# Two small transformers in one launch: first block on feature-major tokens, its norm factors applied behind the products, part of the issue order pinned, weight loads four units ahead

## The chip, the cores and the metric

The kernel runs on one core of one Trainium2 chip. The metric is device time in microseconds (us) of one launch, as a median of runs. The engines are TensorE (PE, with its weight loads shown as PEld), VectorE (DVE), ScalarE (ACT), GpSimd (POOL) and SyncE (SP), which issues the loads. "Half" weights, half clock and so on are explained where they come up.

## What is computed

The first network is one block over 256 tokens of width 1024, a gated linear attention (4 heads, key width 128, value width 256) and a squared-ReLU feed-forward of width 4096. Its output is the input of the second network (two layers of latent and context streams with adaptive norms), which makes up the rest of the launch. The change is in the first network and in the hand-over to the second one's context stream:

```
def rms_norm(x, g):
    y = xf * lax.rsqrt(jnp.mean(xf * xf, axis=-1, keepdims=True) + EPS)
    return (y * g.astype(jnp.float32)).astype(x.dtype)

x = x + gla_mixer(rms_norm(x, norm_mix), ...)
x = x + sqrelu_mlp(rms_norm(x, norm_ffn), w1, w2)     # square(relu(h @ w1)) @ w2

# gla_mixer
proj = h @ w_in                                       # q, k, v, r, gk_low
log_a = log_sigmoid(gk_low @ w_gk_up + b_gk) / 16
... chunked recurrence with decay exp(cumsum(log_a)), output o per head ...
o = rms_norm(o, g_onorm)
return (o * silu(r)) @ w_out
```

A norm is a factor per token (the reciprocal root) and a factor per feature (the gain g). A product over features commutes with the factor per token.

## The kernel before, in words

All weights stream from DRAM once (some twice) as units of 128 x 1024 floats (512 KB), in the order of the list UNITS. Three helpers handle them:

- `w_load(upto)` (line 143) issues loads on SP into tiles `raw` (5 buffers, line 145).
- `w_split(upto)` (line 150) makes two rounded halves of a unit: `wh` by a cast on ACT (line 157) and `wl = raw - wh` on DVE (line 158). Both come from a pool "w" of 13 buffers.
- `wnext(kind)` (line 162) is called where a unit is used. It asks for loads up to five units past the splits (lines 166 and 169) and for splits two units ahead of use (`cap[0]` is 3).

Every wide product is three products of halves (`mm3`, lines 174 to 176): hi x hi, lo x hi, hi x lo. A unit of form "f" (features out) has 24 products over 256 tokens; a unit "r" or "h" has 12 products over 512 columns. So PE needs wh first and wl one product later.

The order of instructions on each engine is chosen ahead of time by the framework's scheduler from its own timing model, with the source order as priority; it may move an instruction past others.

The first block, in source order: x is loaded token-major (lines 120 to 126), with the identity, the gains `vc` and the gate weights `gkraw`. `normed` (line 198) squares each half on ACT (194), gets the reciprocal root on POOL (185 to 187) and scales on DVE (201). `to_T` (208 to 234) transposes on PE (214), and ACT and DVE write two halves of the feature-major tokens `xT` with the gain applied (221, 222). Then come the gate products `pg` (377), eight units f for queries and keys (383 to 391), between which stand the decay chain (398 to 408: product, absolute value, exp, log) and the decay sums (414, 416), and one step of the modulation work after each odd f. A modulation step loads 512 KB (`p`, 284) into a buffer of the pool "w" and reduces it twice on DVE (304). It belongs to the second network and is spread as filler (`adaA`, `adaB`, `adaC`).

Next are eight units of values, with one step of the attention core per unit: `level_diag`, seven levels and `level_cross` (424 to 477), each a few DVE subtractions (443, 444), two exponentials on ACT (446), multiplications (449, 450), small products on PE (457) and a masked copy (458). Two `gate_half` passes give the gates (520, 521). In the second, `heads_out` (531 to 539) makes the head outputs and `heads_T` (553 to 557) transposes them. The output projection follows (579 to 597), then the norm and the transposes of both token tiles into `hT` (595, 608) and the feed-forward: `tok_up`, and from line 671 the loop over 32 units f, with filler. In that loop the context of the second network is loaded, normed and transposed (683 to 690).

Of the kernel before, what the change touches and what calls it, by code (L numbers as in the profile page):

```python
# [16 lines left out]
P = 128  # L17
D = 1024
# [64 lines left out]
def net(ctx, tc, x, vecs, gk_w, gk_up, g_onorm, wst, final_norm, ctx_in, ada, ada_b, cvec, norm_final,  # L83
        rpb, q_gain, k_gain, cmat, cmask, out):
# [30 lines left out]

    xin = [[t2([512]) for _ in range(2)] for _ in range(NT)]
# [3 lines left out]
    for t in range(NT):  # L120
        for hf in range(2):
            nc.sync.dma_start(out=xin[t][hf], in_=x[t * P:(t + 1) * P, hf * 512:(hf + 1) * 512])
        if t == 0:
            nc.sync.dma_start(out=cm[:, C_IDENT:C_IDENT + P], in_=cmat[:, C_IDENT:C_IDENT + P])
    nc.sync.dma_start(out=vc, in_=vecs)
    nc.sync.dma_start(out=gkraw, in_=gk_w.rearrange("p (k r) -> p k r", r=16))
# [4 lines left out]
    V.tensor_copy(out=identr, in_=ident)  # L131
# [215 lines left out]
    adaB = ada_jobs([(0, v, True) for v in (3, 4, 2)])  # L347
    adaC = ada_jobs([(0, 5, True), (1, 0, True), (1, 1, True)] + [(1, v, False) for v in (3, 4, 2, 5)])


    w_load(4)
    xT = new_T()
    gkT = t2([S])
    V.memset(gkT[0:32, :], 1.0)
    xn = [normed(h) for h in xin]
# [3 lines left out]
    to_T(xn, xT, 0, vc[:, V_MIX0, :])  # L359
    nc.sync.dma_start(out=cm[:, C_TRI:C_END], in_=cmat[:, C_TRI:C_END])  # L360
    for ci in range(2):
        bcast_row(crow[ci], cvec, ci * D, D)
    nc.sync.dma_start(out=bcol, in_=ada_b)
    gkup = t2([512])[0:17, :]
    nc.sync.dma_start(out=gkup, in_=gk_up)
    masks = const([P, len(LEVELS), P], "masks", U8)
    for n in range(2):
        mf = t2([4, P])
        m = min(4, len(LEVELS) - 4 * n)
        nc.sync.dma_start(out=mf[:, 0:m, :], in_=cmask[:, 4 * n:4 * n + m, :])  # L370
        G.tensor_copy(out=masks[:, 4 * n:4 * n + m, :], in_=mf[:, 0:m, :])
    gon = t2([256])
    bcast_row(gon, g_onorm, 0, 256)
# [4 lines left out]
    A.copy(out=gkT[0:16, :], in_=pg[0:16, :S])  # L378
# [3 lines left out]
    las = []  # L382
    for f in range(8):
        u = wnext(("f", "w_in"))
        pq = bank()
        for k in range(KD):
            mm_f(pq[:, :S], u, xT, k, 0, S, k == 0, k == KD - 1)
        if f < 4:
# [3 lines left out]
        if f == 0:  # L392
            for ci in range(2):
                A.activation(out=crow[ci], in_=crow[ci], func=AF.Silu)
        if f == 1:
            pzs, es = [bank(), bank()], [t2([512]), t2([512])]
            for t in range(NT):
                T.matmul(pzs[t], lhsT=gkT[0:17, t * P:(t + 1) * P], rhs=gkup, start=True, stop=True)
        if f == 2:
            for pz, e in zip(pzs, es):  # L400
                A.activation(out=e, in_=pz, func=AF.Abs)
            for e in es:
                A.activation(out=e, in_=e, func=AF.Exp, scale=-1.0)
            for e in es:
                A.activation(out=e, in_=e, func=AF.Ln, bias=1.0)
            for pz, e in zip(pzs, es):
                la = t2([512])
                V.scalar_tensor_tensor(out=la, in0=pz, scalar=0.0, in1=e, op0=ALU.min, op1=ALU.subtract)
                las.append(la)
        if f in (4, 5):  # L410
            t = f - 4
            pb = bank()
            for h in range(4):
                T.matmul(pb[:, h * P:(h + 1) * P], lhsT=las[t][:, h * P:(h + 1) * P], rhs=tri, start=True, stop=True)
            for h in range(2):
                A.copy(out=bT[h][:, :, t * P:(t + 1) * P],
                       in_=pb[:, h * S:(h + 1) * S].rearrange("p (h t) -> p h t", h=2))
        ada_run(adaA) if f % 2 else None
# [74 lines left out]
    for k in range(KD):  # L493
        u = wnext(("r", "w_in", k))
        for t in range(NT):
            mm_r(ac[t], u, xT[k], t, k == 0, k == KD - 1)
        core_step()
    for t in range(NT):
        d = [t2([512]) for _ in range(2)]
        for hf in range(2):  # L500
            A.copy(out=d[hf], in_=ac[t][hf])
# [7 lines left out]
    def gate_half(hf, between):  # L509
# [8 lines left out]
        for t in range(NT):  # L518
            sg[t][hf] = t2([512])
            A.activation(out=sg[t][hf], in_=ac[t], func=AF.Silu)  # L520
            V.tensor_tensor(out=sg[t][hf].rearrange("p (h v) -> p h v", h=2),
                            in0=sg[t][hf].rearrange("p (h v) -> p h v", h=2),
                            in1=gon.rearrange("p (o v) -> p o v", o=1).to_broadcast([P, 2, 256]), op=ALU.mult)

    def heads_out(t):
        ms, rs = sums[t]
        for hf in range(2):
# [6 lines left out]
            for h in (2 * hf, 2 * hf + 1):  # L534
                vs = slice((h % 2) * 256, (h % 2 + 1) * 256)
                A.activation(out=ys[t][hf][:, vs], in_=po[:, vs], func=AF.Square, scale=1.0 / 16.0,
                             accum_out=ms[:, h:h + 1])
# [22 lines left out]
    while core or open_:  # L560
        core_step()

    def second(kp):
# [886 lines left out]
```

## Time and profile before

| what | before |
|---|---|
| median of 3 runs | 1293.06 us (1291.61 to 1294.86) |
| profiled execution: its time, its span | 1293.85 us, 1292.1 us |
| ACT busy | 685.1 us (53%) |
| DMA moved | 228.84 MB |
| raw loads (`raw`), modulation loads (`p`) | 310 and 96, 512 KB each |

The span runs from the first to the last instruction; the time of the execution holds the span and what lies around it. "Busy" of PE counts modelled ends of pipelined products, so products that follow each other without a gap show as one busy stretch even at half the clock; the step from one start to the next shows the speed. In a wait row, "PE b L174 <- DVE t L222: 3.4, 2, 2.1" means: the product of line 174 waited for DVE's line 222, 3.4 us in total, twice, 2.1 us the longest.

### The profile page before, as it was taken

How to read it: one execution, taken by the hardware profiler on the slowest of the kernel's cores; microseconds unless marked ns; L12 is line 12 of the kernel's file. 1: busy time of each engine (PE TensorE's matmuls, PEld its weight loads, DVE VectorE, ACT ScalarE, POOL GpSimd, SP SyncE). 2: the span in 40 equal slices, each digit the busy share in tenths (PEclk: the TensorE clock that was granted, in tenths of full speed). 3: DMA queues.
4: the chain of work that ended last, by engine and by line, in shares of the span. 5: the costliest groups of instructions: out<-in, count | busy, mean ns of one | idle time of the engine just before them, and what ended most of it. 6: DMA issues, size and time to landing. Idle time of an engine off the chain costs nothing. (4 is left out here: it accounts for less than half of the span.)

```text
span 1292.1 us, 18813 instructions
## 1 busy us (share of the span) xinstructions
PE 1256.1 (97%) x6992; PEld 1049.7 (81%) x6992; DVE 920.6 (71%) x1612; ACT 685.1 (53%) x1312; POOL 68.3 (5%) x125
## 2 busy tenths in 40 slices
PE   6999999999999999999999999999999999999997
PEld 5887788998878777789877888888888677899996
DVE  3996798787899778778656666646667877655554
ACT  5655565566538888854212312223556887644442
POOL 1000000010200000010000000000002200000001
PEclk9999999999999999999999999999999999999999
DMA  7626587877575232364755675664853133766650
GB/s 278 228 86 209 173 274 244 281 249 245 196 250 124 83 107 87 104 221 131 167 170 194 219 230 196 222 150 140 291 191 116 48 99 86 225 191 184 196 164 33
DMA packets 73454, 228.84 MB, mean 177 GB/s; under 512 B 14209, under 2 KB 14849, under 8 KB 73362
## 3 DMA queue, kind: packets, MB, share of 16 engines
q1 hardware_dynamic: 73362, 227.64, 55.9%
q8 instruction: 55, 0.90, 0.3%
q14 instruction: 37, 0.30, 0.1%
HBM read 226.54 MB, written 1.07 MB: 176 GB/s over the span
## 5 line engine op out<-in xcount | busy, mean ns | idle before, releaser
L157 ACT CAST wh<-raw 128x1024 fp32r<-128x1024 f32 x310 | 318.9, 1042 | 296.4 <-DVE mod L304 92.9
L158 DVE TENSOR_TENSOR wl<-raw,wh 128x1024 fp32r<-128x1024 f32 x310 | 372.1, 1212 | 141.8 <-PE b L175 75.6
L175 PE MATMUL b<-t,wl 128*128 128x256 f32 (+1 forms) x1120 | 366.5, 327 | 5.6 <-DVE wl L158 5.6
L174 PE MATMUL b<-t,wh 128*128 128x256 f32 (+1 forms) x1120 | 367.2, 328 | 1.5 <-ACT wh L157 1.5
L176 PE MATMUL b<-t,wh 128*128 128x256 f32 (+1 forms) x1120 | 365.6, 327 | 0.0
L174 PE MATMUL b<-wh,t 128*128 128x512 f32 x744 | 296.4, 400 | 5.0 <-DVE t L222 2.1
L175 PE MATMUL b<-wh,t 128*128 128x512 f32 x744 | 295.8, 398 | 0.4 <-DVE t L557 0.2
L176 PE MATMUL b<-wl,t 128*128 128x512 f32 x744 | 294.9, 397 | 0.0
L304 DVE CUSTOM_DVE_ANT_0 p<-p,crow 128x1024 f32<-128x1024 f32 x160 | 194.6, 1222 | 105.0 <-DMA p<-in_ada_dram 100.4
L175 PEld LDWEIGHTS b<-t,wl 128*128 128x128 f32 x1120 | 211.6, 189 | 28.9 <-DVE wl L158 7.3
L174 PEld LDWEIGHTS b<-t,wh 128*128 128x128 f32 x1120 | 211.7, 189 | 24.3 <-ACT wh L157 1.7
L176 PEld LDWEIGHTS b<-t,wh 128*128 128x128 f32 x1120 | 211.4, 189 | 20.3
L174 PEld LDWEIGHTS b<-wh,t 128*128 128x128 f32 x744 | 139.8, 188 | 36.6 <-DVE t L222 2.3
L175 PEld LDWEIGHTS b<-wh,t 128*128 128x128 f32 x744 | 140.0, 188 | 33.1 <-DVE t L1280 1.1
L176 PEld LDWEIGHTS b<-wl,t 128*128 128x128 f32 x744 | 140.0, 188 | 32.8 <-DVE wl L158 0.3
L953 ACT CAST t<-t 128x512 fp32r<-128x512 f32 (+1 forms) x42 | 21.8, 519 | 86.1 <-DVE t L947 86.1
L185 POOL TENSOR_SCALAR c<-c 128x1 f32<-128x1 f32 x22 | 10.6, 482 | 619.1 <-ACT t L194 438.7
L946 ACT ACTIVATE t<-b 128x512 f32<-128x512 f32 (+1 forms) x42 | 20.7, 493 | 42.5 <-PE b L176 42.5
L319 POOL TENSOR_TENSOR mod<-mod,bcol 128x8 f32<-128x8 f32 x20 | 13.9, 695 | 437.0 <-DVE mod L304 433.6
L194 ACT ACTIVATE t<-t 128x512 f32<-128x512 f32 x40 | 25.0, 625 | 21.5 <-DVE t L916 8.7
L954 DVE TENSOR_TENSOR t<-t,t 128x512 fp32r<-128x512 f32 (+1 forms) x42 | 23.7, 564 | 15.4 <-ACT t L953 15.4
L214 PE MATMUL b<-cm,t 128*128 128x128 f32 x144 | 23.7, 294 | 8.7 <-DVE t L201 8.1
(203 smaller groups left out, 1187.3 us busy)
## 6 DMA issues: line engine op xcount, KB each, us to landing
raw<-in_wst_dram SPq DMA_DIRECT2D x310, 512.0 KB, 4.1
p<-in_ada_dram SPq DMA_DIRECT2D x96, 512.0 KB, 4.7
t<-in_rpb_dram SPq DMA_DIRECT2D x16, 256.0 KB, 4.1
t<-row SPq DMA_DIRECT2D x12, 256.0 KB, 6.3
t<-in_ctx_dram SPq DMA_DIRECT2D x8, 256.0 KB, 6.1
t<-in_x_dram SPq DMA_DIRECT2D x4, 256.0 KB, 3.2
crow<-in_cvec_dram SPq DMA_DIRECT2D x2, 512.0 KB, 9.4
out_dram<-t SPq DMA_DIRECT2D x4, 256.0 KB, 2.3
```

The source lines that it names most:

```text
L157: A.copy(out=h[:, :n], in_=raw[:, :n])
L158: V.tensor_tensor(out=l[:, :n], in0=raw[:, :n], in1=h[:, :n], op=ALU.subtract)
L174: T.matmul(o, lhsT=lh, rhs=rh, start=first, stop=False)
L175: T.matmul(o, lhsT=ll, rhs=rh, start=False, stop=False)
L176: T.matmul(o, lhsT=lh, rhs=rl, start=False, stop=last)
L194: A.activation(out=junk[hf], in_=halves[hf], func=AF.Square, scale=1.0 / 32.0, accum_out=ms[:, hf:hf + 1])
L214: T.transpose(out=pt[:, i * P:(i + 1) * P], in_=xn[k // 4][:, (k % 4) * P:(k % 4 + 1) * P], identity=ident)
L304: V.tensor_tensor_reduce(out=raw if ci == n_c - 1 else p4([D]), in0=raw, in1=crow[ci], scale=1.0, scalar=0.0, op0=ALU.mult, op1=ALU.add, a ...
L319: G.tensor_tensor(out=m, in0=m, in1=bcol[:, L, v, :], op=ALU.add)
L946: A.activation(out=a, in_=pa[:, :n], func=AF.Silu)
L953: A.copy(out=h, in_=a)
L954: V.tensor_tensor(out=l, in0=a, in1=h, op=ALU.subtract)
```

## The change

1. Inputs get feature-major copies of x (`xt`) and of the context (`ctxt`). The block's tokens `xT` come from `xt` with the gain alone. The factors per token are computed later (`norm_factors`, after the second unit) into `rx` and applied behind the products: to the decay logits, the values (its square), the gates and the scale of the heads' squares. Queries and keys need none: the head norm behind them takes it out.
2. The decay bias is added on DVE from its own load instead of a row of ones in the product.
3. For SP, ACT and DVE the order up to the end of the eight units is the source order (`tc.manual_schedule`); after that, up to the end of the second gate half, for ACT alone.
4. Loads that the start does not need (masks, gain of the heads, `crow`, ...) move behind unit 5 (`later_operands`); the gate weights and gains are issued by ACT. Modulation steps leave the eight units; two run in the second gate half, the rest in the feed-forward loop up to f = 19. `adaB` takes its jobs in the order 2, 3, 4.
5. The feed-forward's norm: the residual itself is transposed; the squared factor is applied to the last product (ReLU squared lets it through as a square).
6. The context: two transposes make a row of factors, POOL multiplies the feature-major context by it.
7. `w_load` asks for four units past the splits instead of five. The buffers stay five.

```diff
-        w_load(max(i + 1, wpos[1]) + 5)
+        w_load(max(i + 1, wpos[1]) + 4)
...
-            w_load(wpos[1] + 5)
+            w_load(wpos[1] + 4)
...
-    adaB = ada_jobs([(0, v, True) for v in (3, 4, 2)])
+    adaB = ada_jobs([(0, v, True) for v in (2, 3, 4)])
...
+    nc.scalar.dma_start(out=gkraw, in_=gk_w.rearrange("p (k r) -> p k r", r=16))
+    nc.scalar.dma_start(out=vc, in_=vecs)
...
+    in_order = tc.manual_schedule(engines={mybir.EngineType.SP, mybir.EngineType.Activation, mybir.EngineType.DVE})
+    in_order.__enter__()
+    for n in range(KD // 2):
+        nc.sync.dma_start(out=xraw[n], in_=xt[:, 2 * n:2 * n + 2, :])
     w_load(4)
+    for t in range(NT):
+        for hf in range(2):
+            nc.sync.dma_start(out=xin[t][hf], in_=x[t * P:(t + 1) * P, hf * 512:(hf + 1) * 512])
...
-    xn = [normed(h) for h in xin]
...
-    to_T(xn, xT, 0, vc[:, V_MIX0, :])
...
     for k in range(KD):
+        src, w = xraw[k // 2][:, k % 2, :], vc[:, V_MIX0, k:k + 1]
+        A.activation(out=xT[k][0], in_=src, func=AF.Copy, scale=w)
+        V.scalar_tensor_tensor(out=xT[k][1], in0=src, scalar=w, in1=xT[k][0], op0=ALU.mult, op1=ALU.subtract)
         mm3(pg[0:16, :S], gkh[:, k, :], gkl[:, k, :], *xs(xT, k, 0, S), k == 0, k == KD - 1)
...
+    def norm_factors():
+        for t in range(NT):
+            r, _ = rstd_of(xin[t])
+            G.tensor_copy(out=rx[t][:, 0:1], in_=r)
+            G.tensor_tensor(out=rx[t][:, 1:2], in0=r, in1=r, op=ALU.mult)
+            G.tensor_scalar(out=rx[t][:, 2:3], in0=r, scalar1=1.0 / 16.0, scalar2=None, op0=ALU.mult)
...
         if f == 1:
+            norm_factors()
...
         if f == 2:
+            for t in range(NT):
+                V.scalar_tensor_tensor(out=zs[t], in0=pzs[t], scalar=rx[t][:, 0:1], in1=gkbias, op0=ALU.mult,
+                                       op1=ALU.add)
+        if f == 3:
             (absolute value, exp)
+        if f == 4:
             (log, minimum)
+        if f == 5:
+            later_operands()
+        if f == 7:
+            decay_sums(0)
-        ada_run(adaA) if f % 2 else None
+    in_order.__exit__(None, None, None)
+    in_order = tc.manual_schedule(engines={mybir.EngineType.Activation})
+    in_order.__enter__()
...
     def second(kp):
-        if kp < 2:
-            heads_out(kp)
-            gated_heads(kp, 0)
-        if kp == 3:
+        if kp == 0:
+            for t in range(NT):
+                heads_out(t)
+            for t in range(NT):
+                gated_heads(t, 0)
+        if kp == 2:
             heads_T(range(4))
+        if kp in (1, 3):
+            ada_run(adaA)
     gate_half(1, second)
+    in_order.__exit__(None, None, None)
...
             if (t, k) == (1, KD - 1):
-                to_T([xn[0]], hT, 0, vc[:, V_FFN0, :])
+                to_T([xin[0]], hT, 0, vc[:, V_FFN0, :])
...
     def tok_up(src, us, finish):
         for t in range(NT):
-            if t == 1:
-                to_T([xn[t]], src, t * P, *finish[1:])
             o = bank()
             for kp in range(4):
                 if t == 0:
+                    if kp == 3:
+                        to_T([xn[1]], src, P, *finish[1:])
                     us.append(wnext(finish[0]))
...
+    def ctx_parts(rc, scale, bias):
+        pr = bank()
+        for t in range(NT):
+            T.transpose(out=pr[:, t * P:(t + 1) * P], in_=rc[t].to_broadcast([P, P]), identity=ident)
...
+        for k in range(KD):
+            z = cts[k // 2][:, k % 2, :]
+            G.tensor_tensor(out=z, in0=z, in1=rows, op=ALU.mult)
...
-        if f < 14:
+        if f < 20:
             ada_run(adaA) if f % 4 != 3 else None
...
-            xn = [normed(t) for t in hc]
             aT = new_T2()
-            ctx_T = to_T_steps(xn, aT, S, mod(0, 1, 1), mod(0, 1, 0))
+            ctx_T = ctx_parts(rc, mod(0, 1, 1), mod(0, 1, 0))
```

The two lines in brackets above stand for unchanged instructions that moved.

More of the change, by code (lines that the diff above doesn't have):

```diff
@@ L113, in const @@
         return sb.tile(shape, dt, name=name)
+    xraw = [t2([2, S]) for _ in range(KD // 2)]
     xin = [[t2([512]) for _ in range(2)] for _ in range(NT)]
@@ L382, in net, with later_operands @@
-    las = []
+    nc.sync.dma_start(out=gkup[0:16, :], in_=gk_up)
+    nc.sync.dma_start(out=cm[:, :C_COS], in_=cmat[:, :C_COS])
+    bcast_row(gkbias, gk_b, 0, 512)
+    masks = const([P, len(LEVELS), P], "masks", U8)
+    gon = t2([256])
+    def later_operands():
+        for n in range(2):
+            mf = t2([4, P])
+            m = min(4, len(LEVELS) - 4 * n)
+            nc.sync.dma_start(out=mf[:, 0:m, :], in_=cmask[:, 4 * n:4 * n + m, :])
+            G.tensor_copy(out=masks[:, 4 * n:4 * n + m, :], in_=mf[:, 0:m, :])
+        bcast_row(gon, g_onorm, 0, 256)
+        nc.sync.dma_start(out=cm[:, C_COS:], in_=cmat[:, C_COS:])
+        nc.sync.dma_start(out=bcol, in_=ada_b)
+        for ci in range(2):
+            bcast_row(crow[ci], cvec, ci * D, D)
@@ L383, in net, with decay_sums @@
+    def decay_sums(t):
+        pb = bank()
+        for h in range(4):
+            T.matmul(pb[:, h * P:(h + 1) * P], lhsT=las[t][:, h * P:(h + 1) * P], rhs=tri, start=True, stop=True)
+        for h in range(2):
+            A.copy(out=bT[h][:, :, t * P:(t + 1) * P],
+                   in_=pb[:, h * S:(h + 1) * S].rearrange("p (h t) -> p h t", h=2))
     for f in range(8):
@@ L387, in net @@
             mm_f(pq[:, :S], u, xT, k, 0, S, k == 0, k == KD - 1)
+        if f == 0:
+            A.copy(out=gkT[0:16, :], in_=pg[0:16, :S])
         if f < 4:
@@ L698, in net @@
     for t in range(NT):
-        residual(lat[t], ac[t])
+        for hf in range(2):
+            V.scalar_tensor_tensor(out=lat[t][hf], in0=ac[t][hf], scalar=rr[t][:, 0:1], in1=lat[t][hf],
+                                   op0=ALU.mult, op1=ALU.add)
         r, _ = rstd_of(lat[t])
```

114 lines of the change are left out of this document (56 added, 58 removed).

## The prediction, made before the changed kernel ran

> **What bounds the kernel now.** I read the page first, then who TensorE (PE) waited for, then a table by stage.
>
> ```profile
> PE 1256.1 (97%) x6992; PEld 1049.7 (81%) x6992; DVE 920.6 (71%) x1612; ACT 685.1 (53%) x1312; POOL 68.3 (5%) x125
> ```
>
> PE is busy for 97% of the span. An edit elsewhere pays only where it ends a wait of PE, removes products, or keeps PE's clock up. The waits of PE, in total, with times and longest:
>
> ```profile
> PE b L214 <- DVE t L201: 8.1, 2, 6.3
> PE b L174 <- DVE t L222: 3.4, 2, 2.1
> PE b L174 <- ACT t L520: 1.7, 1, 1.7
> ```
>
> These three, the longest but for late weight halves (L157, L158), are waits for the norms, transposes and gates of the first block. By stage (columns: stretch, length, busy time of PE, PEld, DVE, ACT, POOL, clock, DMA):
>
> ```profile
> 34.20:37.70 3.50, 3.50 (x17) 3.50 (x18) 3.22 (x5) 2.79 (x5) 0.00 (x0) 0.51 0.74 227
> 48.87:92.80 43.93, 43.90 (x259) 37.77 (x258) 43.69 (x92) 23.61 (x34) 0.00 (x0) 1.00 0.41 135
> 151.50:160.00 8.50, 8.50 (x50) 7.38 (x51) 7.46 (x16) 3.98 (x6) 0.00 (x0) 1.00 0.72 255
> 160.00:350.00 190.00, 190.00 (x1152) 167.91 (x1152) 153.71 (x219) 113.80 (x195) 14.70 (x24) 1.00 0.76 254
> 350.00:655.00 305.00, 303.67 (x1640) 245.74 (x1639) 240.01 (x551) 193.20 (x446) 10.84 (x18) 1.00 0.48 138
> 655.00:705.00 50.00, 45.86 (x190) 36.10 (x189) 33.55 (x49) 11.09 (x15) 1.44 (x2) 0.97 0.61 210
> ```
>
> From 49 to 93 and from 160 to 350 PE has no gap at all, and little to 655. Its losses sit before 49 us, at two places between 114 and 152 (rows under C), and at 655 to 705. The change reaches the first two directly.
>
> **A: the start.** Timeline rows of before (start, length, engine, line, operation):
>
> ```profile
> 0.72 0.87 SPq L122 DMA_DIRECT2D t<-in_x_dram  x2
> 3.38 0.63 ACT L194 ACTIVATE t<-t 128x512 f32<-128x512 f32 x1 [1.38 <-DMA t<-in_x_dram]
> 3.53 0.43 SPq L126 DMA_DIRECT2D t<-in_gk_w_dram  x1
> 4.00 1.94 SPq L146 DMA_DIRECT2D raw<-in_wst_dram  x4
> 8.01 0.30 ACT L357 CAST t<-t 128x128 fp32r<-128x128 f32 x1 [0.41 <-DMA t<-in_gk_w_dram]
> 10.52 1.05 ACT L157 CAST wh<-raw 128x1024 fp32r<-128x1024 f32 x1 [2.21 <-DMA raw<-in_wst_dram]
> 11.60 1.23 DVE L158 TENSOR_TENSOR wl<-raw,wh 128x1024 fp32r<-128x1024 f32 x1 [1.88 <-ACT wh L157]
> 13.27 0.40 PE L174 MATMUL b<-t,t 128*16 128x256 f32 x1 [1.28 <-DVE t L222]
> 17.09 0.34 PE L174 MATMUL b<-t,t 128*16 128x256 f32 x1
> 17.38 0.28 PE L174 MATMUL b<-t,wh 128*128 128x256 f32 x1
> 46.07 0.37 ACT L391 COPY t<-b 128x256 f32<-128x256 f32 x1 [0.26 <-PE b L176]
> 48.87 0.38 ACT L391 COPY t<-b 128x256 f32<-128x256 f32 x1 [1.47 <-PE b L176]
> ```
>
> Unit 0's weights were split at 12.8 (11.60 + 1.23), but its products start at 17.38: ahead of them stand the squares, the norm, 16 transposes and the 24 gate products, which run at half speed (18 starts from 13.27 to 17.09, 0.212 us each; later a unit of 24 takes 48.87 - 46.07 = 2.80, 0.117 each). The changed kernel needs no norm and no transposes first. The first feature-major tile should land like x, at 3.4. The gate weights, now the first load on ACT's own queue, took 4.5 us from issue to use (3.53 to 8.01) behind x; alone they cannot beat x's 2.7. From 0.72 that gives 3.4 to 5.2, then a 0.30 cast, its difference and a token pair: the gate products start between 4.8 and 6.1, take 24 x 0.212 = 5.1 and end between 9.9 and 11.2.
>
> Unit 0 becomes the bound. The page's median from issue to landing of a weight unit:
>
> ```profile
> raw<-in_wst_dram SPq DMA_DIRECT2D x310, 512.0 KB, 4.1
> ```
>
> Its load is now issued behind four token loads, at 0.72 + 4 x 0.44 = 2.5 instead of 4.0, with about the same bytes ahead. Bounds on its arrival: 10.5, as today, and 6.6 (2.5 + 4.1). I take today's 6.5 us from issue to cast: 9.0 to 9.2. Then wh at 10.2 and wl at 11.5, which the second product needs. Unit 0 starts in earnest at **11.5 instead of 17.4: -5.9**. Arriving as late as today it starts at 12.8, -4.6; arriving at 6.6 it waits for the gate products, near 10, -7.4.
>
> **The clock.** PE idles between the gate products (about 10) and 11.5. Before lost 3.1 us of starts at 31.03 to 34.10 (rows under B), and the clock then stood at 0.51 for 3.5 us; at 148.9 to 151.35 a wait of 2.1 (C) left it at 1.00 (151.50 to 160.00). My 1.5 is nearer to the second, but the start is also where the clock first has to rise. Bounds: 0 and two such stretches of half speed, 2 x 1.7. I take **+0.8**.
>
> **B: units 2 to 7.**
>
> ```profile
> 28.83 1.08 ACT L401 ACTIVATE t<-b 128x512 f32<-128x512 f32 x2
> 29.93 1.28 ACT L403 ACT_TABLE_LOAD   x1
> 31.03 0.28 PE L176 MATMUL b<-t,wh 128*128 128x256 f32 x1
> 31.76 1.03 ACT L157 CAST wh<-raw 128x1024 fp32r<-128x1024 f32 x1
> 34.10 0.46 PE L175 MATMUL b<-t,wl 128*128 128x256 f32 x1 [0.88 <-DVE wl L158]
> 34.63 1.15 ACT L405 ACTIVATE t<-t 128x512 f32<-128x512 f32 x2
> 35.29 1.29 DVE L408 SCALAR_TENSOR_TENSOR t<-b,t 128x512 f32<-128x512 f32 x2
> L398 PE MATMUL b<-t,t 17*128 17x512 f32 x4 | 2.0, 614 | 0.0
> ```
>
> Unit 4's cast stood behind the whole decay chain (absolute value, a table load, an exponential), so PE lost 3.1 - 0.2 = 2.9, and 3.5 us at half speed cost 1.7 more. Source order puts each cast ahead of that step's chain and two units ahead of use: **-4.6**.
>
> It does not make ACT free. Count from E1, the end of unit 1's products. ACT in its fixed order: evict 0.4; four squares with their read-outs, 2.9 (a row of 0.63 + about 0.1 each); cast 4, to E1 + 4.3. Decay products hold PE 2.0, so unit 2 ends at E1 + 4.8 and unit 3 at 7.6. Then evict 3 (8.0), L401 (9.1), table (10.4), exponentials (11.6), cast 6 (12.6), wl 6 (13.8). PE wants unit 6 at E1 + 2.0 + 4 x 2.80 = 13.2: 0.6 late. Then evict 4 (13.0), table (14.3), L405 (15.4), cast 7 (16.5); but DVE, also fixed, does L408's two first (15.4 to 16.8), so wl 7 is at 18.0, wanted at 16.6: 1.4 late: **+2.0** in all (0 if the table is already there, 3.5 if both lags add and the clock drops once). The waiting ACT holds back only evictions, and those banks are not wanted at once.
>
> The four modulation steps that leave this stage take 8 x 1.22 us of DVE and 2 MB of loads with them. They come back after 160 us. I cost that at nothing: DVE is busy 154 of 190 and 240 of 305 us there, PE nearly always. Without that cover it is 9.8. The loads of x, context and their feature-major copies (2 MB more in total) hide below DMA shares of 0.76. SP is in source order too: unit 4's load stands behind fifteen issues, near 7.5 (0.72 + 15 x 0.45), far ahead of its use past 20.
>
> **C: the two places at 114 and 149.**
>
> ```profile
> 113.12 2.07 ACT L157 CAST wh<-raw 128x1024 fp32r<-128x1024 f32 x2 [3.54 <-DVE mod L304]
> 114.14 1.03 PE L553 MATMUL b<-cm,t 128*128 128x128 f32 x8
> 116.15 1.12 ACT L520 ACTIVATE t<-b 128x512 f32<-128x512 f32 x2
> 151.35 0.50 PE L174 MATMUL b<-wh,t 128*128 128x512 f32 x1 [2.13 <-DVE t L222]
> ```
>
> At 114.9 PE waits 1.7 for a bank that Silu (L520) frees late, behind casts held by DVE's modulation (L304). The change transposes these heads one weight unit earlier and lets Silu follow its products directly: **-1.7** (0 if DVE still stalls on a modulation load, which the change issues in just these units). At 148.9 the second token tile's transposes wait for the norm; in the change they read the raw residual inside the next products: **-2.1** (about 0.5 stays if the splits of that moment keep DVE). Factor work (scales on existing activations, squares after the up product) is on ACT and POOL beside PE; its last use is 180 us later.
>
> **D: the context.** 16 transposes become 2. Eight of that form take 1.03 in a row at 114.14, at most 0.129 a step, and by my estimate 0.11 without the last one's drain; PE has 190.00 of 190 busy there: 14 x 0.11 = **-1.5**. POOL's eight new products of 256 columns are not in this trace; the nearest has 64:
>
> ```profile
> L1030 POOL TENSOR_TENSOR cgq<-cm,gq x2: 323/324/325, 29.3 to 30.0; 128x64 f32<-128x64 f32 x2
> ```
>
> So 0.3 to 1.3 each, spread over eleven steps of 5.6 us: 0. The Trainium skill, "SBUF — State Buffer", "Who interferes with whom", says that a VectorE instruction with two SBUF inputs and a GpSimd one that reads SBUF exclude each other. By it DVE would wait at most 8 x 1.3 here, out of some 36 idle us; the sum stays.
>
> **Sum.** -5.9 + 0.8 - 4.6 + 2.0 - 1.7 - 2.1 - 1.5 = -13.0. The profiled execution (1293.85 for a span of 1292.1; what lies around it stays) gives 1280.9; the median shown, 1293.06, is 0.8 lower, so I forecast **1280.1**. About 0.3%, 3.9 us, is what a measurement here can tell from no change.
>
> **The rivals.** Rows: SP's waits, who waited for modulation loads, DVE's first and last instruction of the decay levels.
>
> ```profile
> SPq L146 <- DVE wl L158: 740.1, 243, 17.9
>   DVE p L304: 100.4, 31
> 56.29 1.28 DVE L432 TENSOR_TENSOR t<-b,cm 128x512 f32<-128x512 f32 x2
> 91.80 0.42 DVE L470 TENSOR_TENSOR t<-t,t 128x256 f32<-128x256 f32 x1
> ```
>
> *Fixed ACT order starves the decay levels: slower.* From 48.87 to 92.80 DVE is busy 43.69 of 43.93, just level with PE. In the change ACT is fixed there too: each level's two exponentials (1.3; L401's 128x512 pair took 1.08) queue behind a cast (1.05), and DVE's next multiply behind them. Say DVE idles d per level, for eight steps. DVE's level work runs from 56.29 to 92.2, 36 us, and may start 4.5 after the first value unit does (2.80, the decay sums and ACT's copies of them), so some 3.5 of the 43.9 are spare: the loss is 8d - 3.5. It decides the sign beyond d = 2.6 (loss 17.3). The ceiling of d is cast, exponentials and a level's sixteen short products on PE (0.11 each), 1.05 + 1.3 + 1.75 = 4.1: 1309. At d = 3 it gives 1300.6. Against it: before, the same chain left DVE no idle time, as another level's subtractions fill it. Chance 0.11; a milder d near 2 returns to within 0.3%, with the next rival 0.10.
>
> *Given back later.* Modulation steps pushed past 350 us meet fewer idle slots: at most 9.8 lost, 1289.9. Chance 0.12 for a loss of 4 or more (1284 to 1290).
>
> *Four ahead frees SyncE.* SP's queue sat 740 us behind raw slots, and DVE 100 us behind modulation loads queued there; the waits at 655 to 705 (4.1 idle plus 1.5 of clock) follow from that. If a load that no longer waits for its own slot lets those loads pass, 5.6 more: 1274.5. But five slots stay, so the edit may well do nothing; I leave it at 0. Chance 0.12.
>
> *Clock stays low at the start:* two half-speed stretches, 3.4 in place of 0.8: 1282.7, inside the range. The Trainium skill, "TensorE: Matmul & The Clock Gate", Part 1, gives a free-running window of about 3.4 us, busy to open and idle to close. By it the idle 1.5 closes nothing, but the opening can fall late. This trace disagrees on closing: under 3.1 us with one product inside sufficed.
>
> **Chances.** Forecast (1275 to 1284) 0.55; the others as above. Faster 0.55 + 0.12 + 0.12 = 0.79, same 0.10, slower 0.11. The range, leaving out the slower case and the edge of "same": **1270 to 1290**.
>
> **What would show it.** Right: first wide product near 10 to 12 us; eight units with no wait over 1.5; no half clock after 20 us; value units starting 8 or 9 us earlier; PE 190.00-like between 55 and 150; 14 fewer transposes near 290. Wrong: DVE waiting for ACT exponentials inside the levels, casts of weights late behind squares, or new PE waits after 350.

## The result, and the profile after

| | before | after |
|---|---|---|
| median | 1292.76 us (1289.90 to 1294.86, 10 runs) | 1288.05 us (1283.50 to 1292.56, 10 runs) |
| ratio | | 0.9963, interval 0.9946 to 0.9980 |
| profiled execution: time, span | 1293.85, 1292.1 | 1283.50, 1281.7 |

The kernel became faster, by 4.7 us where 13.0 were forecast. The profiled execution of after is the fastest of its ten, and that of before is 1.1 us above its median. So the two traces differ by 10.4 us, and the trace of after shows less loss than the median holds. One statement ahead of the prediction has to be put right: queries and keys do need their factors. The keys' factor is the second one in the square on the values, and that of the queries is in the gates and in the scale of the heads' squares.

First the start of after, as timeline rows (start, length, engine, line, operation). They answer to the rows under A.

```profile
4.66 0.30 ACT L362 CAST t<-t 128x128 fp32r<-128x128 f32 x1 [1.74 <-DMA t<-in_gk_w_dram]
6.43 0.39 PE L170 MATMUL b<-t,t 128*16 128x256 f32 x1 [6.43 <-ACT t L367]
9.08 2.92 ACT L153 CAST wh<-raw 128x1024 fp32r<-128x1024 f32 x3
10.14 3.50 DVE L154 TENSOR_TENSOR wl<-raw,wh 128x1024 fp32r<-128x1024 f32 x3 [0.45 <-ACT wh L153]
11.60 0.40 PE L170 MATMUL b<-t,wh 128*128 128x256 f32 x2
36.27 0.37 ACT L421 COPY t<-b 128x256 f32<-128x256 f32 x1 [0.87 <-PE b L172]
```

Unit 0's cast is at 9.08, and its second half is done by 11.4. The gate products run without a pause from 6.43, and unit 0's products follow them at 11.60. The last of the eight units is evicted at 36.27 and not at 48.87. The table by stage answers to that of before (stretch, length, busy time of PE, PEld, DVE, ACT, POOL, clock, DMA share, GB/s):

```profile
11.40:35.90 24.50, 24.43 (x197) 23.26 (x196) 13.86 (x15) 17.93 (x32) 8.51 (x16) 1.00 0.84 307
150.00:350.00 200.00, 200.00 (x1191) 175.85 (x1191) 159.56 (x227) 119.41 (x207) 26.97 (x37) 1.00 0.81 246
350.00:370.00 20.00, 12.98 (x48) 9.77 (x47) 16.54 (x26) 4.01 (x5) 1.12 (x1) 0.83 0.78 281
655.00:705.00 50.00, 49.29 (x212) 39.31 (x211) 36.84 (x54) 12.04 (x16) 1.45 (x2) 1.00 0.62 215
```

The stretch 350 to 370 in before:

```profile
350.00:370.00 20.00, 20.00 (x96) 16.25 (x95) 18.29 (x37) 9.39 (x19) 2.34 (x2) 1.00 0.62 186
```

Two things are to be seen. The first eight units run without a stall (24.43 of 24.50). And a hole stands at 350 to 370 that before does not have: 7 us without PE, and the clock at 0.83. The waits of PE in after, first from 0 to 150, then from 330 to 375:

```profile
PE b L170 <- ACT t L367: 6.4, 1, 6.4
PE b L489 <- DVE t L482: 2.2, 1, 2.2
PE b L210 <- DVE t L616: 0.3, 1, 0.3
PE b L170 <- ACT t L664: 0.3, 1, 0.3
```

```profile
PE b L172 <- DVE wl L154: 4.2, 1, 4.2
PE b L170 <- ACT wh L153: 2.9, 1, 2.9
```

The first row is the start. The second is a new wait at 70.8, inside the levels. The row counts it from the modelled end of the product before. From one start to the next it is 2.69 us, where 0.23 is usual, so 2.46 are lost; the waits at 70 are counted in this way from here on. The last two are the hole: weight halves come late. Their chain is read backwards. ACT's casts and DVE's splits stand behind the modulation step's reduces (L300), and the reduce that begins at 353.36 waited 9.34 us for its load `p`.

```profile
353.36 1.23 DVE L300 CUSTOM_DVE_ANT_0 p<-p,crow 128x1024 f32<-128x1024 f32 x1 [9.34 <-DMA p<-in_ada_dram]
...
357.04 1.04 ACT L153 CAST wh<-raw 128x1024 fp32r<-128x1024 f32 x1 [6.75 <-DVE mod L300]
```

So the question is why loads are late there. SP's queue and the DMA page of after, 334 to 350:

```profile
331.65 0.39 SPq L323 DMA_DIRECT2D row<-mod  x1
332.13 0.53 SPq L142 DMA_DIRECT2D raw<-in_wst_dram  x1
...
334.06 0.38 SPq L323 DMA_DIRECT2D row<-mod  x1
336.59 0.33 SPq L142 DMA_DIRECT2D raw<-in_wst_dram  x1
...
344.48 0.33 SPq L132 DMA_DIRECT2D t<-row  x1
```

```profile
DMA packets 2065, 1.48 MB, mean 93 GB/s; under 512 B 1641, under 2 KB 1641, under 8 KB 2065
...
q1 hardware_dynamic: 2065, 1.48, 102.1%
...
raw<-in_wst_dram SPq DMA_DIRECT2D x1, 512.0 KB, 13.6
row<-mod SPq DMA_DIRECT2D x1, 4.0 KB, 14.5
```

The engines of DMA are full (102.1%) while only 93 GB/s move. Four of five packets are small: they are the gate rows. A gate vector of 1024 numbers lies over 128 partitions and is written to DRAM number by number, so one 4 KB row is 1024 packets of 4 bytes. The row took 14.5 us to land, and a weight load issued behind it 13.6, where 4.1 is the page's median of before. The order (2, 3, 4) of `adaB` finishes vector 2 first, and vector 2 is the one whose rows are written.

To follow the gain along the kernel, take copies of one line in both traces (L723 before, L797 after).

```profile
349.61 1.28 ACT L723 COPY t<-b 128x512 f32<-128x512 f32 x2 [1.23 <-PE b L176]
...
374.08 1.29 ACT L723 COPY t<-b 128x512 f32<-128x512 f32 x2 [5.47 <-PE b L176]
```

```profile
335.88 1.28 ACT L797 COPY t<-b 128x512 f32<-128x512 f32 x2 [0.82 <-PE b L172]
...
369.34 1.28 ACT L797 COPY t<-b 128x512 f32<-128x512 f32 x2 [6.43 <-PE b L172]
```

After is 13.7 us ahead at the first and 4.7 at the second. Nine microseconds are lost in between. (Before loses 0.8 itself right behind this point, so the lead is 5.6 at 381, and 8.1 are lost for good.)

### The profile page after: what moved, and what is told of

The parts are those of the page before. It is cut to its first block, busy times and chain, and to the rows that moved or that the text cites. A ratio compares the mean times of both kernels' runs of the same rounds, so it can differ in the third digit from the quotient of the medians.

```text
span 1281.7 us, 18772 instructions
## 1 busy us (share of the span) xinstructions
PE 1249.4 (97%) x6962; PEld 1043.4 (81%) x6962; DVE 919.6 (72%) x1601; ACT 683.6 (53%) x1311; POOL 88.2 (7%) x143
## 5 line engine op out<-in xcount | busy, mean ns | idle before, releaser
L300 DVE CUSTOM_DVE_ANT_0 p<-p,crow 128x1024 f32<-128x1024 f32 x160 | 195.1, 1224 | 108.8 <-DMA p<-in_ada_dram 103.1
L315 POOL TENSOR_TENSOR mod<-mod,bcol 128x8 f32<-128x8 f32 x20 | 17.2, 858 | 512.9 <-DVE mod L300 414.3
L190 ACT ACTIVATE t<-t 128x512 f32<-128x512 f32 x40 | 24.9, 624 | 12.4 <-DVE t L990 8.2
L1021 DVE TENSOR_TENSOR t<-b,t 128x512 f32<-128x512 f32 (+1 forms) x42 | 23.4, 557 | 6.1 <-PE b L172 6.1
```

The lines of the kernel that those rows point to most:

```text
L190: A.activation(out=junk[hf], in_=halves[hf], func=AF.Square, scale=1.0 / 32.0, accum_out=ms[:, hf:hf + 1])
L300: V.tensor_tensor_reduce(out=raw if ci == n_c - 1 else p4([D]), in0=raw, in1=crow[ci], scale=1.0, scalar=0.0, op0=ALU.mult, op1=ALU.add, a ...
L315: G.tensor_tensor(out=m, in0=m, in1=bcol[:, L, v, :], op=ALU.add)
L1021: V.tensor_tensor(out=a, in0=pg_[:, :n], in1=a, op=ALU.mult)
```

## The experiments

### Where the nine microseconds at 350 go

The changed kernel once more, beside the next three:

> The changed kernel once more, to see whether its spread (1283.5 to 1292.6 us in ten runs, where the kernel before has 1289.9 to 1294.9) is of one place. Theory 'rows': PE waits some 7 us near 355 to 363 us, because the gate rows of the second network (1024 packets of 4 bytes each) now travel in the middle of the value units, and how often the clock halves after such waits differs from run to run. It expects a median near 1288, again 5 us or more between runs, the wait near 355 in the profile, and more half-clock time near it when the run is slow. Rival 'start': the spread comes from the opening of the clock in the first 20 us; then the profile shows slow products there in a slow run and the wait near 355 unchanged.

1286.03 us, ratio 0.9951 (0.9932 to 0.9969). The waits at 355 are there again, 3.4 and 4.9 us, and the one at 70. This profile is 2.5 us longer than that of after. It is up to 0.5 us ahead of it near 70, 1.1 behind at 93, after a half clock, and some 2 more behind at 370. So the rival "start" falls.

**The order put back** (`e1_order_back`):

```diff
-    adaB = ada_jobs([(0, v, True) for v in (2, 3, 4)])
+    adaB = ada_jobs([(0, v, True) for v in (3, 4, 2)])
```

> The changed kernel with the modulation jobs of adaB in the order 3, 4, 2 again; nothing else. Theory 'rows': the row writes leave the value stage, the wait near 355 falls from 7.3 us to about the 0.8 of the kernel before, and with the half clock behind it the median falls by 7 to 9 us, to 1279 to 1281. Rival 'late steps': the wait comes from the modulation loads that moved from before f = 14 to after f = 20, in whatever order; then the wait and the median (1288) stay within 2 us. Rival 'elsewhere': the rows return further on and cost as much there: 1286 to 1288 with a new wait after 380 us.

1277.15 us, ratio 0.9877 (0.9863 to 0.9891): 8.9 us less than after beside it. The rows of vector 2 are now written at 465.6, in the attention stage. The stretch 350 to 370:

```profile
350.00:370.00 20.00, 19.41 (x83) 15.16 (x82) 19.28 (x33) 7.91 (x12) 2.24 (x2) 1.00 0.72 238
```

The hole is gone (19.41 of 20.00, clock 1.00). One line of the diff cost 8.9 us of the 15.3 that the rest brings (1292.4 before, beside these runs). The spread shrinks too: 3.2 us over four runs, where after beside it has 9.8 over seven.

**The steps put back in time, order kept** (`e2_timing_back`): in the feed-forward loop `if f < 20` becomes `if f < 14` again, and the rows are written at 281.6.

> The changed kernel with adaA running only up to f = 13 in the feed-forward loop and adaB from f = 14, as before; the order of adaB stays 2, 3, 4. Theory 'rows': the gate rows are written earlier, in the feed-forward loop, at some 300 us, where PE had 190.00 of 190 us busy; whether loads then come late there is open, but the wait near 355 shrinks, to 1280 to 1285. Rival 'late steps': the wait vanishes wholly since four fewer steps stand in the value stage: 1279 to 1281, the same as with the order put back.

1281.15 us, ratio 0.9911 (0.9893 to 0.9928). The hole is spread: some 2 us at 306 to 311 and 3.0 at 341 to 344. This profile is the slowest of six runs. By the medians, half of the loss (4.9 of 8.9) hangs on when the steps run, and 4.0 stay.

**The order alone, in the kernel before** (`e4_before_order`): (2, 3, 4) in place of (3, 4, 2).

> The kernel before with only the order of adaB changed, to 2, 3, 4. There the jobs run some 30 us earlier against the value stage, so the rows are written in the feed-forward loop. Theory 'rows' in its plain form (any row write beside modulation loads costs PE 7 us) expects 1297 to 1300; if it needs the value stage, 1291 to 1295. Rival 'late steps': no change, 1291 to 1295.

1292.30 us, ratio 0.9995 (0.9981 to 1.0008). Rows written at 289.95 make no wait of PE over 0.5 us up to 420. So the order costs nothing in the kernel before. In the changed kernel it costs 8.9 with the later steps and 4.0 without them (`e2_timing_back` against `e1_order_back`). Which other part of the change makes up those 4.0 is not shown.

**Packets or order?** (`e6_rows_by_pe`): order and steps as in after, but the row leaves in 8 packets.

```diff
-                nc.sync.dma_start(out=rows[ci].rearrange("(k p) -> p k", p=P), in_=modc[(L, ci, v)])
+                pt, rw = bank(), t2([512])
+                T.transpose(out=pt[0:KD, 0:P], in_=modc[(L, ci, v)], identity=ident)
+                V.tensor_copy(out=rw[0:KD, 0:P], in_=pt[0:KD, 0:P])
+                nc.sync.dma_start(out=rows[ci].rearrange("(k p) -> k p", p=P), in_=rw[0:KD, 0:P])
```

> The changed kernel with its order of the modulation vectors (2, 3, 4) kept, and each gate vector turned on PE (one transpose, one copy by DVE) before it is written, so that a row leaves as 8 packets of 512 bytes and not as 1024 of 4 bytes. Theory SMALL PACKETS (the two rows written amid the value stage fill the DMA queues, raw loads and modulation loads behind them come late, PE waits at 355): the waits of 3.0 and 4.3 us and the half clock after them go, and the time is near that of the order put back, 1277 to 1281, ratio 0.988 to 0.991. Theory ORDER (where the steps fall counts, or SP stands behind the reading of a row until its writing has landed, whatever the packets): the waits near 355 stay, time 1284 to 1288, ratio 0.993 to 0.997.

1279.42 us, ratio 0.9901 (0.9887 to 0.9916). The DMA page of this run, 334 to 350:

```profile
DMA packets 1061, 3.16 MB, mean 198 GB/s; under 512 B 123, under 2 KB 139, under 8 KB 1061
...
q1 hardware_dynamic: 1061, 3.16, 59.2%
...
raw<-in_wst_dram SPq DMA_DIRECT2D x1, 512.0 KB, 3.7
```

Half the packets carry twice the bytes at 59.2%, and the raw load lands in 3.7 us. Small packets made the hole. A rest of 1.9 us stays at 357, where after had 7.1. The rows are still read back there, 1 MB in all, amid the modulation loads; that this makes the rest is not shown.

**Or SP, standing behind the reading of a row?** (`e7_rows_read_late`): six steps, not one, between writing and reading.

```diff
-            yield
+            for _ in range(6):
+                yield
```

> The changed kernel with the reading back of each gate row six steps behind its writing, not one, so that SP never stands behind a row that is still being written; packets stay at 4 bytes. Theory SP BLOCKED (the loads behind the waiting read are what is late): the waits near 355 go, 1277 to 1281, ratio 0.988 to 0.991. Theory SMALL PACKETS (the queues themselves are full): a wait of 2 us or more stays between 340 and 365, time 1282 to 1288, ratio 0.992 to 0.997. The longer job also spreads its steps over more of the value stage, which either theory costs at nothing, but the last of them may then fall into the attention stage.

1288.09 us, ratio 0.9963 (0.9949 to 0.9978): nothing gained. The waits of this run from 330 to 375:

```profile
PE b L172 <- DVE wl L154: 3.9, 1, 3.9
PE b L170 <- ACT wh L153: 1.9, 1, 1.9
```

SP no longer stands behind a row that is being written (9.8 us in after), and PE waits as before: from 334 to 350 a weight load still takes 15.1 us to land and a row 16.4. The theory of the blocked queue falls.

### The waits between 655 and 705

The trace of after gains 5 us more there than was forecast (49.29 busy of 50, before 45.86, and no half clock).

**Four ahead alone** (`e5_before_four`): the kernel before with `+ 4` for `+ 5` in both lines of `wnext`.

> The kernel before with only its raw weight loads issued four units ahead, not five. Rival of the prediction FOUR AHEAD FREES SYNCE: the waits of 2.8 and 1.3 us between 655 and 705 and the half clock after them go, 1287 to 1289, ratio 0.995 to 0.998. Theory NOTHING (five slots stay, and a load that waits no more for its own slot waits for the next thing): 1292 to 1294, ratio 0.999 to 1.001. Theory LESS LOOKAHEAD (a late load has one unit less to hide behind): 1294 to 1298, ratio 1.001 to 1.004.

1292.61 us, ratio 1.0003 (0.9993 to 1.0014). A wait of 2.4 us stays at 693 with a half clock behind it. The rival "Four ahead frees SyncE" falls, in the kernel before.

**The rows of before turned on PE** (`e13_before_rows_pe`), the edit of `e6_rows_by_pe` in the kernel before:

> The kernel before with every gate row turned on PE and written in 8 packets of 512 bytes, nothing else. Theory SMALL PACKETS EVERYWHERE: the waits at 661 and 696 (4.1 us) and the half clock after 696 (1.7 us) go, 1286.5 to 1289, ratio 0.995 to 0.997. Theory ONLY THE VALUE STAGE (the late weight halves there come from something else): a wait of 2 us or more stays between 655 and 705, 1291 to 1294, ratio 0.999 to 1.001.

1286.89 us, ratio 0.9958 (0.9944 to 0.9972): 5.0 us from this alone, more than the whole change brought. The stretch:

```profile
655.00:705.00 50.00, 50.00 (x216) 40.17 (x215) 38.72 (x60) 14.32 (x18) 1.89 (x3) 1.00 0.67 225
```

So writing the rows of 4-byte packets also made these waits, though the chain between them was not followed. In before two rows are issued at 625.04 and 628.42, and the weight loads from 622 to 646 take 14.9 us to land (median of three). In the run with turned rows they take 5.6 in that stretch and 3.6 from 650 to 675, where its rows are written. SP issues nothing from 629.1 to 644.08, and the first wait of PE comes at 661. The turned rows are also written later (655.41) and read back earlier (658.60 in place of 685.66), and this run does not separate that from the packets. Why the waits are shorter in after, with the packets unchanged, no run singles out. Its weight loads behind the rows are nearly as slow (12.4), and the waits were 2.4 in `e2_timing_back`, 0.9 in after and 1.0 with the order put back, so I take it for a matter of which loads happen to meet the rows.

**Both** (`e12_order_and_pe`), the order put back and the rows turned:

> The changed kernel with the modulation vectors in the order of before, and every gate row turned on PE and written in 8 packets of 512 bytes. Theory SMALL PACKETS EVERYWHERE (the waits at 372 to 375 and at 655 to 705 follow rows of 1024 packets as well): the 1.0 to 1.2 us at 683 goes, none is left between 340 and 400, and the time is 1275.5 to 1277, about 1 us below the order alone; PE pays some 0.1 us for each turned row. Theory ONLY THE VALUE STAGE: the same as the order alone, 1277 to 1278.

1276.93 us, ratio 0.9883 (0.9868 to 0.9898). The wait of 1.0 at 683 is gone (50.00 busy of 50); against the order alone the difference is too small to measure.

### The fixed order and the wait at 70

**No fixed order** (`e9_no_pins`): the order of `adaB` put back, both `tc.manual_schedule` blocks removed.

> The changed kernel with the modulation vectors in the order of before, and with no fixed order at all: the scheduler places ACT, DVE and SP work in the first block as in the rest. Theory SOURCE ORDER PAYS (unit 4's cast behind the decay chain, Silu behind the casts, was the scheduler's doing): 4 to 8 us of the gain goes, 1281 to 1285, with a wait of 2 to 3 us near unit 4 or 5 of the first stage. Theory FEATURE-MAJOR ALONE (the first unit starts early because norms and transposes no longer stand ahead of it, and the rest follows): within 2 us of the fixed order, 1275 to 1279. Theory FIXED ORDER STARVES THE LEVELS (the rival of the prediction, mild): faster than the fixed order, the wait at 70 gone, 1273 to 1275.

1281.34 us, ratio 0.9918 (0.9905 to 0.9931), some 4 us slower than with the fixed order. Its start and its waits to 150:

```profile
10.40 1.04 ACT L153 CAST wh<-raw 128x1024 fp32r<-128x1024 f32 x1 [4.39 <-DMA raw<-in_wst_dram]
11.68 1.04 ACT L153 CAST wh<-raw 128x1024 fp32r<-128x1024 f32 x1 [0.24 <-DMA raw<-in_wst_dram]
12.97 1.04 ACT L153 CAST wh<-raw 128x1024 fp32r<-128x1024 f32 x1 [0.24 <-DMA raw<-in_wst_dram]
13.92 0.29 ACT L360 CAST t<-t 128x128 fp32r<-128x128 f32 x1
...
14.67 0.40 PE L170 MATMUL b<-t,t 128*16 128x256 f32 x1 [14.67 <-ACT t L365]
```

Left free, the scheduler puts four weight casts ahead of the gate weights' cast (the first, at 4.97, is not shown) and PE starts at 14.67 in place of 6.4: 8 us. No wait stands at unit 4 or at 70. So the order at the start buys 8 us, and by 150 half of them are given back. The wait and the half clock at 70 take 4.2 in the profile of `e1_order_back`; the rest of the way was not followed. The time is in the range of "Source order pays", but the wait near unit 4 or 5 that this theory expected is not there.

**Decay sums earlier** (`e8_decay_early`): on top of the order put back, `decay_sums` at f = 6 and 7, none behind the first value unit.

> The changed kernel with the modulation vectors in the order of before, and the decay sums of both tiles issued in the first stage (units 6 and 7), not one of them behind the first value unit. Theory LEVELS BOUND BY DVE (the levels start 2.8 us late on a DVE that is then busy without a gap, and PE catches it up at 70.8): the wait of 2.46 us at 70 and the half clock behind it in some executions go: 1.5 to 4 us less than with the order alone, 1273.2 to 1275.7, ratio 0.985 to 0.987. Theory FIXED ORDER (the wait is made by casts, exponentials and evictions that stand in one fixed order on ACT): the wait stays within 0.5 us of 2.46, time 1276.5 to 1278, or more if the sums come later than unit 7's casts on DVE want.

1276.59 us, ratio 0.9881 (0.9865 to 0.9896); the wait is still 2.47. **The whole chain a unit earlier** (`e11_core_early`): besides that, one `core_step()` ahead of the value loop.

> The changed kernel with the modulation vectors in the order of before, the decay sums of both tiles in the first stage, and the chain of diagonal and levels begun one value unit earlier, fixed order kept. Theory DVE BOUND (the chain has to start earlier, nothing else): the first level work on DVE starts near 40 and not 46, the wait at 70 goes, 1273 to 1275. Theory FIXED ORDER ON ACT: a wait of 2 us or more stays, at 65 to 71, 1276 to 1278.

1277.02 us, ratio 0.9887 (0.9868 to 0.9906). DVE's level work starts at 42.6 and not at 46.0, and still a wait of 2.8 stands at 72. It is now a level later in the chain, but at the same time. An early start of the chain is not the point.

**Fixed order for the first eight units only** (`e10_first_pin`): the order put back, the second `tc.manual_schedule` removed.

> The changed kernel with the modulation vectors in the order of before, and the fixed order kept for the first eight units only (SP, ACT, DVE), not for ACT in the value, level and gate stage. Theory FIXED ORDER ON ACT MAKES THE WAIT AT 70 (weight casts queued behind exponentials leave TensorE's list with one weight product between two levels): the wait of 2.46 us and the half clock after it go, 1273 to 1275.5, ratio 0.985 to 0.9865. Theory DVE BOUND (DVE works without a gap from 46 to 74, 5.05 us a level, and TensorE comes to the levels 9 us earlier than before): a wait of 2 to 3 us stays, 1276.5 to 1278. If the fixed order also bought the 1.7 us at Silu (114.9 in before), that wait comes back and takes 1.7 of either.

1276.28 us, ratio 0.9881 (0.9865 to 0.9897). 1.1 us are left at 70, but 1.3 appear at 104. It settles neither theory.

**Two units more split ahead** (`e14_split_ahead`): on `e12_order_and_pe`, `cap[0]` rises to 5 during the levels.

> The changed kernel with the modulation vectors in the order of before, gate rows turned on PE, and from the seventh unit to the end of the levels two units more split ahead of use (five, not three). Theory SUPPLY OF SPLIT UNITS (TensorE uses 14 products of weights a level and gets 12, one unit a level): the wait of 2.46 us at 70 and the half clock after it go, 1272.5 to 1275, ratio 0.985 to 0.9865. Theory DVE BOUND (5.05 us of DVE work a level): a wait of 2 us or more stays between 65 and 80, or comes later, near 90, where the level chain ends, 1276 to 1278.

1275.45 us, ratio 0.9890 (0.9866 to 0.9913), and a wait of 2.6 at 71. The same with the fixed order for eight units only (`e15_first_pin_ahead`):

> The same with five split ahead and rows turned on PE, and the fixed order kept for the first eight units only. Theory SUPPLY OF SPLIT UNITS: without ACT's fixed order the scheduler places the casts early anyway, so the waits of 1.1 at 70 and 1.3 at 104 shrink by less than in the fixed order, 1273 to 1276. Theory DVE BOUND: both stay, 1275.5 to 1277.

1277.76 us, ratio 0.9893 (0.9874 to 0.9911), a wait of 2.6 at 71.5. The supply of split units falls too. What is left is PE's own list. Timeline of PE in after:

```profile
69.12 1.95 PE L489 MATMUL b<-t 128*128 128x128 f32 x16
70.83 0.48 PE L172 MATMUL b<-wl,t 128*128 128x512 f32 x1
73.52 1.13 PE L489 MATMUL b<-t 128*128 128x128 f32 x8 [2.22 <-DVE t L482]
```

Between earlier levels stand 14 weight products, here one: the 96 products of the eight value units are used up. DVE needs 5.05 us a level (with the order put back its weight splits among them start at 49.39, 54.43 and 59.48), and PE comes to the next one after 16 products and one.

**A gate unit between the two levels** (`e16_gate_first` on `e14_split_ahead`, `e17_gate_first_three` on `e12_order_and_pe`):

```diff
-        core_step()
+        if k < KD - 1:
+            core_step()
```

> The run with five units split ahead (order of before, rows turned on PE), with no level step behind the eighth value unit, so that the first gate unit's 12 products stand between two levels. Theory END OF THE VALUE UNITS (TensorE has run out of value products by 71 and its list has two levels in a row there): the wait of 2.6 us goes, or stays under 0.8, 1272 to 1274, ratio 0.985 to 0.987. Theory DVE BOUND (22.00 of 22.00 us busy, whatever TensorE does between): the 2 us or more come back within the next 20 us, 1275 to 1277.

> The same edit on the run with three units split ahead (order of before, rows turned on PE). Theory END OF THE VALUE UNITS, with the supply of split units enough: the wait of 2.46 us goes, 1273 to 1275. Theory SUPPLY AS WELL: the first gate unit is not yet split there (its cast is at 73.3), so a wait of 1 to 2.5 us stays at 71, now for a weight half, 1275 to 1277.

1271.70 us, ratio 0.9843 (0.9825 to 0.9860), and 1273.18 us, ratio 0.9855 (0.9837 to 0.9873). The stretches of `e16_gate_first`:

```profile
50.00:72.00 22.00, 22.00 (x132) 19.24 (x131) 22.00 (x48) 8.87 (x13) 0.00 (x0) 1.00 0.36 98
72.00:95.00 23.00, 23.00 (x123) 19.80 (x122) 19.06 (x36) 17.69 (x34) 0.55 (x2) 1.00 0.54 181
```

DVE is as full as ever (22.00 of 22.00) and PE no longer waits. So the wait came from the list running out of value products while DVE still needed its 5.05 us, and DVE's rate alone did not make it. With three units split ahead the wait is gone as well, so "Supply as well" falls; the two units more are still worth 1.5 us (the slowest execution with five ahead took 1271.84, the fastest with three 1272.44). `e16_gate_first` is the fastest version, 20 us below before (1291.38 beside it). Besides the change it holds the order put back, the rows turned on PE, the units split further ahead, and the level step left out.

## Why the prediction was wrong, step by step

- **A, the start, -5.9.** The size is right: 11.60 in place of 17.38 is -5.8. The path was only in part the one that I told, so some of the hit is luck. The gate products began at 6.43, later than the 4.8 to 6.1 that I gave as bounds, because the first piece of `xT` waited 0.9 us for the gains `vc`, the second load on ACT's queue, which I had left out. They ended near 11.6, just behind unit 0's split, so they and not unit 0 were the bound.
- **The clock, +0.8.** Not seen: the idle time between the gate products and unit 0, on which the term stood, did not occur, and the clock is 1.00 from 11.40 on.
- **B, -4.6 and +2.0.** The -4.6 came, as PE has no wait at unit 4. That source order is the reason is not shown: `e9_no_pins` has no fixed order and no wait there either. Both it and after spread the decay chain over units 3 and 4 and have no modulation steps there. The +2.0 did not come; the eight units have no wait (24.43 of 24.50). ACT's rows show why:

```profile
25.01 1.14 ACT L434 ACTIVATE t<-t 128x512 f32<-128x512 f32 x2
26.05 1.14 ACT L436 ACTIVATE t<-t 128x512 f32<-128x512 f32 x2
27.09 1.04 ACT L153 CAST wh<-raw 128x1024 fp32r<-128x1024 f32 x1
28.03 0.37 ACT L421 COPY t<-b 128x256 f32<-128x256 f32 x1
28.41 1.28 ACT L439 ACT_TABLE_LOAD   x1
```

  Absolute value and exponential follow each other with no table load between them; I had put 1.3 us there. Unit 6 was cast 9.8 us after the end of unit 1's products (17.3) and not 11.6, and all later casts move up with it. The 0 that I gave as an end of the term is what came.
- **C, -1.7 and -2.1.** Right in kind. The two waits are gone, and 0.3 twice is left in the rows of after.
- **D, -1.5.** Right as far as the traces show: the 16 transposes between 240 and 330 (3.05 us of modelled busy time) are gone, and the lead grows from 12.2 us (an activation at 183.32 is at 171.14) to 13.7 at 350. POOL's eight products took 0.7 to 1.7 us each, the longest beyond the 1.3 that I gave, and PE had no gap (200.00 of 200).
- **The step that failed: the modulation steps that come back after 160, "I cost that at nothing".** The cover that I named, idle time of DVE, was there; I counted DVE's reduces and the 2 MB of loads and not the rows' writing, which `adaB` in its new order puts into the value stage. It cost 9.0 us in the profile (8.1 by 381) and 8.9 in the timed runs (1286.03 against 1277.15). The order of `adaB` stood in the diff and had no term. The order alone would not have failed the forecast (`e4_before_order`, no loss); it did so together with the later steps and what else had changed. The rival "Given back later" had the place and the ceiling (9.8) nearly right, for another reason: not scarcer idle slots on DVE, but DMA engines full of 4-byte packets.
- **The rival of starved levels.** Its sign was right and its mechanism wrong. The price was 2.5 us, with the half clock 4.2 in some executions. DVE did not wait for exponentials (in after, too, it is busy 22.00 of 22.00 us from 50 to 72); PE's list ran dry.
- **655 to 705.** The lead grows from 5.6 us (an activation at 584.01 is at 578.41) to 10.8 (929.48 against 918.70). The prediction offered 5.6 for it as a rival and named the wrong cause; turned rows take these waits away in the kernel before.

With the order put back the change gives 1277.15, 15.3 us below before, where the sum foretold 13.0. That the two are close is partly luck: the 2.8 us of the clock and of late units did not come, the wait at 70 took 2.5 to 4.2 that were not in the sum, and 655 to 705 gave some 4 to 5 that were not in it either. The sizes of A, C and D and the -4.6 of B were good, and one term was missing.

## What to carry to other kernels

When steps are moved, list every DMA that they issue with its packet size, not only its bytes: 4 KB in 4-byte pieces took three times as long to land as a load of 512 KB (12.4 against 4.1 us, medians of before) and held up the loads behind them. Where one engine's list alternates between two chains, count whether the filler products last as long as the chain; where they end first, give the next stage's products a place in between. A change of many parts should be run with each incidental line put back: here one of them ate 8.9 of 15.

## What the runs showed of the hardware

The six rows of 1024 packets of 4 bytes that the kernel before writes (L327) take this long to land:

```profile
DMA to landing us min/median/max: 9.6/12.4/26.0
```

In after, with two of them in flight, the DMA engines were at 102.1% for 93 GB/s. The Trainium skill, "DMA: Bandwidth & Descriptors", "Rules for kernel authors", says that a strided last dimension becomes one descriptor per element and should be rearranged; the trace agrees, 1641 of 2065 packets being under 512 bytes, and gives the price that the rule leaves open.

The same wait of 2.46 us at 70 left the clock at 1.00 in the profile of after and halved it for 3.4 us in others. Of ten profiles with this wait (2.69 to 2.73 from start to start), five show 1.00 from 74 to 78 and five 0.57 to 0.63. After, then after once more:

```profile
70.00:80.00 10.00, 7.78 (x53) 6.83 (x52) 9.19 (x20) 4.76 (x8) 0.00 (x0) 1.00 0.33 105
```

```profile
70.00:80.00 10.00, 7.79 (x38) 6.73 (x37) 8.90 (x20) 4.14 (x7) 0.00 (x0) 0.83 0.33 105
```

PE's busy time is the same and its count differs, 53 products against 38. So a wait of this length costs 2.5 or 4.2 us, and no run shows what decides which. I take this for a part of the spread of after's runs.
